# A short product ahead of each sum of products in a hybrid RG-LRU, pooling and Conformer block

## The chip, the cores and the metric

The kernel runs on one core of one Trainium2 chip. The metric is the device time of one execution in microseconds (us). Two runs of the kernel before are shown, 990.06 and 989.09 us; their median is 989.58 us.

## The reference

One layer works on 256 latent tokens and 256 context tokens of 2048 channels. Both are RMS-normalised and modulated by a shift and a scale that come from the condition vectors through `w_ada`. An input projection `w_in` gives seven groups of 1024 columns and three groups of 2048 gate logits:

```python
cols = split(h @ w_in)                        # xa, za, xb, zb, cv, cg, zc, gl
ya = rglru_both_directions(conv4(cols.xa))    # starts from the context's last state
yb = multiscale_pool(cols.xb) ; yc = conformer_conv(cols.cv, cols.cg)   # yc ends in @ w_pwc
acc = sum_k sigmoid(gl[k]) * ((y[k] * silu(z[k])) @ w_bout[k])
out = x + gate * (acc @ w_out + b_out)        # then a last RMS norm over the channels
```

The context takes part only in `xa`. All arithmetic is held to float32, so the kernel writes each operand of a large product as a high and a low part in the format float32r and adds three products: high by high, high by low, low by high.

## The kernel before

The main sequence (the loop `for kind, key, item, q in steps`) is a list of steps, each with one weight piece of 1 MB that the SP queue loads into one of three slots of `raws`. ScalarE writes the high part of a piece (`wh`, line 84) and VectorE the low part (`wl`, line 210), for the next step while TensorE works on this one. Between the splits VectorE runs background chains (convolutions, scan, layer norm, the gate) as far as a step's planned time of 5.1 us has room.

The kinds of steps are: one `xa` step (512 columns of tokens), 48 branch steps (`xb`, `zb`, `cv`, `cg`, `za`, `zc`, eight of each), 48 gate-logit steps (`gl`), 24 projection steps (`bout`), 4 steps of the pointwise convolution (`pwc`) and 16 `out` steps. All but `out` hand their work to one helper, `columns`, as jobs. A job is one sum over k: the weights are the stationary operand, 128 by 128, and the tokens the moving one, 256 columns. For each k it runs the high weights against the high tokens (line 249) and against the low tokens (line 250); when the high parts of all jobs are done, it runs the low weights against the high tokens (line 253). A branch or gate-logit step is one job with 16 values of k, 48 products. A projection step calls `columns` twice, each time with one job of 8 values of k, 24 products. A `pwc` step calls it once with two jobs of 8. The sums of one step go to PSUM banks that ScalarE and VectorE read out in the next step.

Between the steps stand a few other products on TensorE: those of the RG-LRU gates (`mm3`, lines 239 to 241, 512 columns), those of the pooling mixer (`mm3`, 256 columns), and six sums over the partitions with a matrix `ones` in plain float32 (lines 731, 745 and 940). Before the main sequence, phase 1 streams `w_ada` (line 390, 32 stationary columns), turns the sums with products of two columns (lines 398 and 399) and multiplies the first seven tiles of `xa` (`mm3`, 512 columns).

The order on TensorE is the order in which the program emits products; nothing is moved around. The change touches only `columns` and one line of the main loop.

Of the kernel before, what the change touches and what calls it, by code (L numbers as in the profile page):

```python
# [23 lines left out]

# column offsets inside the packed per-channel vectors
V_G, V_BSH, V_BSC = 0, 16, 32
# [6 lines left out]

# arena offsets (float32 per partition)
A_SQ0, A_XT, A_H, A_S, A_RAW = 0, 8192, 16384, 17408, 17920
# [11 lines left out]
class Feed:  # L47
    """Weight pieces of 8 KB per partition: loaded ahead into slots, and split into two float32r parts."""

# [41 lines left out]
class Background:  # L91
    """Elementwise chains cut into small steps that fill the vector engine between weight splits.

    A chain is a list of named generators that run one after another. Each yields None after what it has just
    emitted, "S" where the next part has to wait for the next weight piece, or a function that says whether the
    next part may be emitted (in a tuple where that is only better so)."""

# [7 lines left out]
    def _step(self, chain):  # L105
        """Emits the next part; False if it can't be emitted yet."""
        if chain["until"] is not None:
            if not chain["until"]():
                return False
            chain["until"] = None  # L110
        try:
            r = next(chain["parts"][0][1])
        except StopIteration:
            self.done.add(chain["parts"].pop(0)[0])
            if not chain["parts"]:
                self.chains.remove(chain)
            return True
        chain["soft"] = isinstance(r, tuple)
        if chain["soft"]:
            r = r[0]  # L120
        if callable(r):
            chain["until"] = r
        return r != "S"
# [22 lines left out]
def hybrid_block_kernel(  # L146
# [91 lines left out]
    def mm3(ps, sh, sl, mh, ml, start, stop):  # L238
        T.matmul(ps, sh, mh, start=start, stop=False)  # L239
        T.matmul(ps, sh, ml, start=False, stop=False)  # L240
        T.matmul(ps, sl, mh, start=False, stop=stop)  # L241

    def columns(jobs):
        """Sums over k of weights (stationary) times tokens (moving) in three float32r products each; those
        with the low part of the weights come last, so that it may be late. A job: output, high and low parts
        of the weights per k, high and low parts of the tokens per k."""
        for ps, wh, wl, mh, ml in jobs:
            for k in range(len(wh)):
                T.matmul(ps, wh[k], mh[k], start=k == 0, stop=False)  # L249
                T.matmul(ps, wh[k], ml[k], start=False, stop=False)  # L250
        for ps, wh, wl, mh, ml in jobs:
            for k in range(len(wh)):
                T.matmul(ps, wl[k], mh[k], start=False, stop=k == len(wh) - 1)  # L253

    def tiles128(parts):
        """The 128-column tiles of a split piece, high and low."""
        return [[part[i][:, P * k:P * (k + 1)] for part in parts for k in range(8)] for i in range(2)]

    def rsqrt_newton(o, v, tmp, r):
        """o = 1/sqrt(v): square root, reciprocal, one Newton step."""  # L260
        A.activation(r, v, AF.Sqrt)
        recip(r, r)
        tt(tmp, r, r, ALU.mult)
        tt(tmp, tmp, v, ALU.mult)
        ts(tmp, tmp, -0.5, 1.5)
        tt(o, tmp, r, ALU.mult)

    feed = Feed(nc, whp, wlp)

    # order of the weight pieces  # L270
    main_slots = [(f"m{i}", raws[:, i, :]) for i in range(3)]
# [25 lines left out]
    steps = []  # L297
# [57 lines left out]
    with tc.manual_schedule():  # L355
# [1 line left out]
        cin = sml[:, 0:32]  # L357
# [18 lines left out]
        rows = ar[:, A_RB:A_RB + 512]  # L376
# [41 lines left out]
        def keep_warm(n):  # L418
            """Products that nothing reads: the tensor engine's clock halves when it has been idle."""
            for _ in range(n):  # L420
                T.matmul(warm, ones, xT[:, 10, :], start=True, stop=True)

# [1 line left out]
        fold = ar[:, A_XS:A_XS + 512]  # L424
# [35 lines left out]

# [1 line left out]
        xa_ps = [bank() for _ in range(6)] + [small_bank() for _ in range(NXA - 6)]  # L462
# [18 lines left out]

# [1 line left out]
        xap = [ar[:, A_XAP + 518 * t:A_XAP + 518 * (t + 1)].rearrange("p (s l) -> p s l", s=2) for t in range(8)]  # L483
# [12 lines left out]
        gth = [ar[:, A_GTH + 512 * i:A_GTH + 512 * (i + 1)] for i in range(2)]  # L496
        # context halves of the split modulated tokens, free after xa: products' operands of the branches
        cH, cL = hH[:, :, 256:512], hL[:, :, 256:512]
# [11 lines left out]

# [1 line left out]
        nsp, tsp, brh, bih = sml[:, 96:112], sml[:, 112:128], sml[:, 128:144], sml[:, 144:160]  # L512

        def prep():
            """softplus(-lam) = max(-lam, 0) + log1p(exp(-|lam|)); log1p(e) = 2 atanh(e / (2 + e))."""
            lam = vt[:, V_LAM:V_LAM + 16]
            e, z, q, s = sml[:, 0:16], sml[:, 16:32], sml[:, 32:48], sml[:, 48:64]
            ts(brh, vt[:, V_BR:V_BR + 16], 0.5, None)
            ts(bih, vt[:, V_BI:V_BI + 16], 0.5, None)
            ts(q, lam, -1.0, None)  # L520
            tt(e, lam, q, ALU.min)
            A.activation(e, e, AF.Exp)
            ts(s, q, 0.0, None, op0=ALU.max)
            yield
            ts(z, e, 2.0, None, op0=ALU.add)
            recip(z, z)
            tt(z, z, e, ALU.mult)
            yield
            tt(q, z, z, ALU.mult)
            ts(e, q, 1.0 / 19, 1.0 / 17)  # L530
            for m in (15, 13, 11, 9, 7, 5, 3, 1):
                tt(e, e, q, ALU.mult)
                ts(e, e, 1.0 / m, None, op0=ALU.add)
                yield
            tt(e, e, z, ALU.mult)
            stt(s, e, 2.0, s, ALU.mult, ALU.add)
            ts(nsp, s, -4.0, None)
            ts(tsp, s, 2.0, None)
            yield
            ts(vt[:, V_PS:V_PS + 8], vt[:, V_PS:V_PS + 8], 0.5, None)  # L540
            ts(vt[:, V_CCW:V_CCW + 248], vt[:, V_CCW:V_CCW + 248], 0.5, None)
            ts(vt[:, V_PB:V_PB + 8], vt[:, V_PB:V_PB + 8], 0.5, None)
            yield
# [4 lines left out]
        def conv_a(pr):  # L548
            """Two heads: depthwise convolution of width 4, then the two parts of the result."""
            hd = (2 * pr, 2 * pr + 1)  # L550
# [229 lines left out]

# [1 line left out]
        G.memset(ar[:, A_XAP:A_XAP + 4144], 0.0)  # L782
# [15 lines left out]
        def silu_parts(ps):  # L798
            """(1 + tanh(z / 2)) z, twice silu(z)."""
            th = take("th", th_t)  # L800
            A.activation(th, ps[:, 0:256], AF.Tanh, scale=0.5)
            return th
# [69 lines left out]
        def merge_end(k, j):  # L872
            """Two channel tiles of a branch into the sum; after the last branch, half the sum in two parts."""
            a = acc[:, j, :]
# [29 lines left out]
        def gate_chunk(n):  # L904
            """The gate on every partition: silu(c) times the weight rows of each partition, then the sum over
            the partitions; and x + gate * b_out."""
            c = slice(512 * n, 512 * (n + 1))
# [63 lines left out]
        def finish(t, halves):  # L971
            """The last chunk of a token tile, then the RMS norm over its rows; the first three chunks are
            multiplied by final_g already."""
            var, r, tmp = [sml[:, 16 + 4 * t + i:17 + 4 * t + i] for i in range(3)]
# [25 lines left out]

# [1 line left out]
        first, later, post = [], [], []  # L1002
        step_no = [0]
        avail = load["V"]
        for kind, key, item, q in steps:
# [12 lines left out]
            for f in due:  # L1018
                f()
            parts = it["parts"]  # L1020

            if kind in ("xa", "xb", "zb", "cv", "cg", "za", "zc"):
# [31 lines left out]
            elif kind == "out":  # L1054
# [10 lines left out]
                def out_mm(t, ps, lo, hi, qs, low):  # L1065
                    """One token tile: tokens stationary, weights moving; the low part of the weights last."""
                    tk = slice(P * t, P * (t + 1))
# [60 lines left out]
def _layout(inputs):  # L1128
    """Arrays in the order in which the kernel reads them: permutations, slices and concatenations only."""
    f = {k: np.asarray(v, dtype=np.float32) for k, v in inputs.items()}  # L1130
# [58 lines left out]
```

## Time and profile before

| what | value |
|---|---|
| median of the two runs | 989.58 us |
| span of the profiled execution, first to last instruction | 990.5 us |
| TensorE busy | 965.3 us (97% of the span), 7528 products |
| VectorE busy | 743.6 us (75%) |
| ScalarE busy | 493.0 us (50%) |
| mean granted TensorE clock | 0.993 |
| DMA | 220.70 MB, mean 223 GB/s |

No device time is given for the profiled execution beside its span; the span is 0.9 us over the median of the runs. In the trace a product on TensorE has a record of its own (PE) and so has the load of its weights (PEld). The length of a product's record holds its way through the pipeline and overlaps the next record, so the time that a product really costs is read from start to start, over many products, and is called its pace here.

### The profile page before, as it was taken

The page shows a single profiled execution, that of the slowest core. Times are in us where ns is not written, and L with a number is a line of the kernel's source. Part 1 is how long each engine was busy: PE and PEld are TensorE (multiplying, and loading weights), DVE is VectorE, ACT ScalarE, POOL GpSimd, SP SyncE. Part 2 cuts the span into 40 slices and gives each one's busy share as a digit, 9 for nine tenths or more (in the row PEclk, how much of TensorE's full clock was granted, in tenths as well). Part 3 has the DMA queues.
Part 4 walks back from the last instruction along what each step waited for, and adds up shares of the span by engine and source line. Part 5 has one row for each costly group of instructions (what it writes and reads, how often), then busy time and mean ns, then how long its engine had stood idle before and what let it go on. Part 6 is the DMA issues. An engine that isn't in the chain of part 4 may idle for free.

```text
span 990.5 us, 18090 instructions
## 1 busy us (share of the span) xinstructions
PE 965.3 (97%) x7528; PEld 893.6 (90%) x7528; DVE 743.6 (75%) x1143; ACT 493.0 (50%) x641; POOL 40.6 (4%) x74
## 2 busy tenths in 40 slices
PE   4999999999999999999999999999999999999996
PEld 1566668999999999999999999999999999998885
DVE  5445456866976775889899899896756788998864
ACT  4212226566656767674444533444565464454442
POOL 0000010000100000000000000000002111101000
PEclk9999999999999999999999999999999999999998
DMA  9897854544545555444555545555468789878652
GB/s 373 322 418 313 359 194 162 211 171 167 181 163 182 182 181 178 174 171 170 203 181 176 200 178 191 193 173 175 169 216 342 256 301 331 326 249 303 214 178 85
DMA packets 34722, 220.70 MB, mean 223 GB/s; under 512 B 4128, under 2 KB 4272, under 8 KB 11856
## 3 DMA queue, kind: packets, MB, share of 16 engines
q1 hardware_dynamic: 28080, 195.28, 54.1%
q0 software_dynamic: 6560, 24.26, 7.2%
q8 instruction: 59, 0.97, 0.4%
q14 instruction: 23, 0.19, 0.1%
HBM read 217.43 MB, written 2.10 MB: 222 GB/s over the span
## 4 chain that ended last, share of the span: by engine, by line
PE 96%; DVE 2%; ACT 1%; DMA 1%; issue 0%; ACTq 0%; SPq 0%; DVEq 0%
PE acc L253 24%; PE acc L250 24%; PE acc L249 24%; PE sm L390 3%; PE acc L239 3%; PE acc L1075 3%; PE acc L1077 3%; PE acc L1078 3%; PE acc L240 2%; PE acc L241 2%; DVE ar L210 1%; PE sm L240 1%; PE sm L239 1%; PE sm L241 1%; DMA ar<-in_xt_dram 1%; PE sm L399 0%
## 5 line engine op out<-in xcount | busy, mean ns | idle before, releaser
L249 PE MATMUL acc<-hH,wh 128*128 128x256 f32 (+1 forms) x2000 | 479.2, 282 | 0.0
L250 PE MATMUL acc<-hL,wh 128*128 128x256 f32 (+1 forms) x2000 | 477.7, 281 | 0.0
L84 ACT CAST wh<-raws 128x1024 fp32r<-128x1024 f32 (+1 forms) x288 | 297.8, 1048 | 274.8 <-PE acc L250 186.6
L210 DVE TENSOR_TENSOR wl<-raws,wh 128x1024 fp32r<-128x1024 f32 (+1 forms) x288 | 339.6, 1217 | 120.9 <-issue 58.5
L250 PEld LDWEIGHTS acc<-hL,wh 128*128 128x128 f32 x2000 | 378.0, 189 | 2.1 <-issue 0.7
L249 PEld LDWEIGHTS acc<-hH,wh 128*128 128x128 f32 x2000 | 377.5, 189 | 2.1 <-issue 0.7
L253 PE MATMUL acc<-hH,wl 128*128 128x256 f32 (+1 forms) x2000 | 260.3, 281 | 0.0
L253 PEld LDWEIGHTS acc<-hH,wl 128*128 128x128 f32 x2000 | 245.8, 189 | 0.7
L221 DVE SCALAR_TENSOR_TENSOR ar<-ar,vt 128x256 f32<-128x256 f32 (+1 forms) x264 | 115.2, 501 | 0.0
L210 DVE TENSOR_TENSOR ar<-ar 128x512 f32<-128x512 f32 (+6 forms) x136 | 87.3, 664 | 7.9 <-ACT ar L430 6.2
L221 DVE SCALAR_TENSOR_TENSOR ar<-ar,sc 128x512 f32<-128x512 f32 x64 | 48.0, 750 | 17.5 <-DMA ar<-in_w_gate_dram 16.1
L235 ACT CAST hH<-ar 128x256 fp32r<-128x256 f32 (+1 forms) x68 | 31.5, 491 | 54.2 <-DVE ar L217 46.9
L210 DVE TENSOR_TENSOR hL<-ar,hH 128x256 fp32r<-128x256 f32 (+1 forms) x76 | 39.5, 546 | 23.1 <-ACT hH L235 23.1
L1077 PE MATMUL acc<-wh,hH 128*128 128x512 f32 (+1 forms) x144 | 51.8, 369 | 0.0
L1078 PE MATMUL acc<-wh,hL 128*128 128x512 f32 (+1 forms) x144 | 51.3, 366 | 0.0
L239 PE MATMUL acc<-hH,wh 128*128 128x512 f32 x96 | 42.7, 445 | 1.2 <-ACT hH L235 1.2
L215 DVE TENSOR_SCALAR sml<-sm,vt 128x2 f32<-128x2 f32 x16 | 3.5, 219 | 50.8 <-PE sm L399 50.8
L240 PE MATMUL acc<-hL,wh 128*128 128x512 f32 x96 | 38.6, 403 | 0.3 <-DVE hL L210 0.2
L241 PE MATMUL acc<-hH,wl 128*128 128x512 f32 x96 | 38.4, 400 | 0.0
L239 PEld LDWEIGHTS acc<-hH,wh 128*128 128x128 f32 x96 | 18.2, 190 | 16.1 <-issue 12.0
L1075 PE MATMUL acc<-wl,hH 128*128 128x512 f32 (+1 forms) x144 | 32.1, 366 | 0.0
L1078 PEld LDWEIGHTS acc<-wh,hL 128*128 128x128 f32 x144 | 27.0, 188 | 4.8 <-issue 0.2
(136 smaller groups left out, 649.8 us busy)
## 6 DMA issues: line engine op xcount, KB each, us to landing
raws<-in_w_br_dram SPq DMA_DIRECT2D x49, 1024.0 KB, 4.9
raws<-in_w_gl_dram SPq DMA_DIRECT2D x48, 1024.0 KB, 4.9
raws<-in_w_bout_dram SPq DMA_DIRECT2D x24, 1024.0 KB, 4.9
raws<-in_w_ada_dram SPq DMA_DIRECT2D x16, 1024.0 KB, 8.9
ar<-in_w_ada_dram SPq DMA_DIRECT2D x16, 1024.0 KB, 8.3
ar<-in_w_gate_dram POOLq DMA_DIRECT2D x32, 512.0 KB, 6.6
raws<-in_w_out_dram SPq DMA_DIRECT2D x16, 1024.0 KB, 5.0
ar<-in_w_xa_dram SPq DMA_DIRECT2D x5, 896.0 KB, 11.5
```

The lines of the kernel that those rows point to most:

```text
L84: self.nc.scalar.copy(h[:, 0:w], src)
L210: V.tensor_tensor(out=o, in0=a, in1=b, op=op)
L221: V.scalar_tensor_tensor(o, a, s, b, op0=op0, op1=op1)
L239: T.matmul(ps, sh, mh, start=start, stop=False)
L240: T.matmul(ps, sh, ml, start=False, stop=False)
L241: T.matmul(ps, sl, mh, start=False, stop=stop)
L249: T.matmul(ps, wh[k], mh[k], start=k == 0, stop=False)
L250: T.matmul(ps, wh[k], ml[k], start=False, stop=False)
L253: T.matmul(ps, wl[k], mh[k], start=False, stop=k == len(wh) - 1)
L1075: T.matmul(ps, H, wl[:, w], start=False, stop=kt == KT - 1)
L1077: T.matmul(ps, H, wh[:, w], start=kt == 0, stop=False)
L1078: T.matmul(ps, Lo, wh[:, w], start=False, stop=False)
```

## The change

`columns` gets a switch. While it is on, each job begins with one more product: the first high weight tile against the first n columns of the first high token tile, written to the first n columns of the job's own PSUM area with `start=True, stop=True`. The job's first regular product, with `start=True`, writes the same area anew, so nothing of the short product is left in the sum. The widths n go round through 15 values, from 16 to 240 in steps of 16. The switch is set at every step of the main loop, off for `xa` and on for all others; `out` steps don't call `columns`. Phase 1 is untouched. The diff also empties comments and docstrings, which are left out here.

```diff
+LEADS = (32, 64, 96, 128, 160, 192, 224, 16, 48, 80, 112, 144, 176, 208, 240)
...
+    lead = {"on": False, "i": 0}
+
     def columns(jobs):
         for ps, wh, wl, mh, ml in jobs:
+            if lead["on"]:
+                n = LEADS[lead["i"] % len(LEADS)]
+                lead["i"] += 1
+                T.matmul(ps[:, 0:n], wh[0], mh[0][:, 0:n], start=True, stop=True)
             for k in range(len(wh)):
                 T.matmul(ps, wh[k], mh[k], start=k == 0, stop=False)
                 T.matmul(ps, wh[k], ml[k], start=False, stop=False)
...
             parts = it["parts"]
+            lead["on"] = kind != "xa"
```

## Rows read from the trace of the kernel before

**Rows 1.** The page: busy time, granted clock by slice, shares of the last chain.

```profile
PE 965.3 (97%) x7528; PEld 893.6 (90%) x7528; DVE 743.6 (75%) x1143; ACT 493.0 (50%) x641; POOL 40.6 (4%) x74
...
PEclk9999999999999999999999999999999999999998
...
PE 96%; DVE 2%; ACT 1%; DMA 1%; issue 0%; ACTq 0%; SPq 0%; DVEq 0%
```

**Rows 2.** Waits of PE: line, releaser: us in total, times, longest us.

```profile
PE acc L421 <- DMA ar<-in_xt_dram: 12.7, 1, 12.7
PE acc L239 <- ACT hH L235: 1.2, 1, 1.2
PE acc L443 <- DVE ar L210: 1.0, 1, 1.0
PE sm L390 <- DVE sml L217: 0.4, 1, 0.4
PE acc L240 <- DVE hL L210: 0.2, 1, 0.2
```

**Rows 3.** Groups by line and shape, PE: count | busy us, mean ns | idle.

```profile
L249 PE MATMUL acc<-hH,wh 128*128 128x256 f32 x1984 | 472.9, 281 | 0.0
L250 PE MATMUL acc<-hL,wh 128*128 128x256 f32 x1984 | 471.3, 280 | 0.0
L253 PE MATMUL acc<-hH,wl 128*128 128x256 f32 x1984 | 256.4, 280 | 0.0
```

**Rows 4.** The same view, weight loads (PEld) of line 250.

```profile
L250 PEld LDWEIGHTS acc<-hL,wh 128*128 128x128 f32 x2000 | 378.0, 189 | 2.1 <-issue 0.7
```

**Rows 5.** Windows, PE: from:to us, length, busy (products), clock, DMA share, GB/s.

```profile
163.75:190.95 27.20, 27.20 (x241) 1.00 0.61 217
...
433.71:682.46 248.75, 248.75 (x2113) 1.00 0.53 187
683.02:704.67 21.65, 21.65 (x193) 1.00 0.55 186
705.22:789.90 84.68, 84.68 (x721) 1.00 0.70 250
790.88:834.30 43.42, 43.42 (x386) 1.00 0.83 302
...
875.71:891.92 16.21, 16.21 (x145) 1.00 0.68 222
```

**Rows 6.** Timeline of PE in phase 1: start us, us, line, shape, count.

```profile
49.52 0.39 PE L241 MATMUL acc<-hH,wl 128*128 128x512 f32 x1
49.75 0.28 PE L398 MATMUL sm<-sel,ar 128*128 128x2 f32 x2
49.89 0.36 PE L399 MATMUL sm<-sel,ar 128*128 128x2 f32 x2
50.11 0.48 PE L239 MATMUL acc<-hH,wh 128*128 128x512 f32 x1
50.43 0.39 PE L240 MATMUL acc<-hL,wh 128*128 128x512 f32 x1
50.66 0.40 PE L241 MATMUL acc<-hH,wl 128*128 128x512 f32 x1
50.90 0.39 PE L239 MATMUL acc<-hH,wh 128*128 128x512 f32 x1
```

**Rows 7.** Timeline of PE: the first of twelve pooling products, the product after them.

```profile
190.96 0.28 PE L239 MATMUL acc<-hH 128*128 128x256 f32 x1
...
192.39 0.28 PE L249 MATMUL acc<-hH,wh 128*128 128x256 f32 x1
```

**Rows 8.** Timeline of PE: float32 products of `ones` between the windows.

```profile
682.46 0.60 PE L731 MATMUL acc<-ar,ones 128*128 128x256 f32 x2
...
704.67 0.59 PE L745 MATMUL acc<-ar,ones 128*128 128x256 f32 x2
...
789.90 1.02 PE L940 MATMUL acc<-ar,ones 128*128 128x512 f32 x2
```

## The prediction

> **What bounds the kernel now.** I read the page first. TensorE is busy for 97% of the span, the chain that ended last is 96% TensorE, and the granted clock stands at full speed in nearly all slices [rows 1]. The view of waits says where TensorE is not busy: five waits, 12.7 + 1.2 + 1.0 + 0.4 + 0.2 = 15.5 us, all on lines of phase 1 [rows 2]. The steps that the change touches hold no idle time of TensorE (0.0 at each of their three groups [rows 3]). So the kernel is a queue of products, and a product added there lengthens it by what it costs; nothing hides it, and no other engine's wait is ahead of it. The short product needs the weights, the tokens and the PSUM area that the product behind it needs anyway, so it adds no wait of its own. VectorE, ScalarE and the weight loads from memory get more time per step than they have now.
>
> The view that decides is the one that gives the pace of the products. Lines 249, 250 and 253 run 3 x 1984 = 5952 products of 256 columns [rows 3]. Their records are 280 ns long and overlap, so I take windows that begin and end with a product's start and hold these products alone, and divide (the count of a window includes the one or two records that reach into it; steps of 48 give the exact one). The result is not one pace but two [rows 5]. From 433.71 to 682.46 us 2112 products take 248.75 us, 117.8 ns each; 705.22 to 789.90 gives the same (84.68 us by 719). From 163.75 to 190.95, 240 products take 27.20 us, 113.3 ns each; so do the windows from 683.02 (191), 790.88 (383) and 875.71 (143). Instructions, shapes and clock (1.00, which is 2.4 GHz) are the same in both. The pace holds for tens of microseconds and changes only where something else stood between the sums: the twelve pooling products, which themselves go at (192.39 - 190.96) / 12 = 119 ns and leave the slow pace behind them [rows 7], or one float32 product with `ones`, at 682.46 (slow to fast), 704.67 (fast to slow), 789.90 (slow to fast) [rows 8]. The fast windows hold 240 + 192 + 384 + 144 = 960 products, whole steps counted; I count the other 4992 as slow. The difference is 4.45 ns a product.
>
> **The change part by part.** It removes and moves nothing. It adds one product to each sum: 48 branch sums, 48 gate-logit sums, 2 x 24 projection sums and 2 x 4 of the pointwise convolution, together 152. Their widths are ten full rounds of the 15 values (1920 columns) and 32 + 64, in all 19296 columns, 127 on average.
>
> What one costs. Every product has a weight load of its own: line 250 loads 2000 times [rows 4], although line 249 just ahead of it used the same tile, so the regular product behind the short one will load again. What a product costs when there is next to nothing to stream is shown in phase 1: from 49.52 to 50.43 us stand two products of 512 columns and four of two columns [rows 6]. The next two products of 512 columns take 50.90 - 50.43 = 0.47 us, so the four short ones take 0.91 - 0.47 = 0.44 us, 110 ns each. That is close to a full product of 256 columns, and the width does not matter up to 240 columns: at the fast pace a column streams in 113.3 / 256 = 0.443 ns, and 240 take 106 ns. I take the pace of the sum that the product leads, 113 to 118 ns, since that row is a plain float32 one and the neighbours are float32r: 152 x 115.6 = 17.6 us. The bounds are 152 x 110 = 16.7 us and, at the pooling products' 119 ns, 18.1 us. The lower end would go to the columns alone, 19296 x 0.443 = 8.5 us, if the second load of the same weights were hidden; that is a rival below.
>
> By the Trainium skill, "TensorE: Matmul & The Clock Gate", section "Back-to-back issue gap", an isolated product of N columns takes N / 2.4 + 2.5 ns, which is an estimate of 152 x 55 = 8.4 us here; the two-column products in the trace disagree with it as a price for products that each load weights.
>
> What it does to the pace. This is the unknown. Each short product is a disturbance like those that changed the pace before: for one product the load of the weights and the streaming are out of step, and the widths make the disturbance different from sum to sum. No row shows a short float32r product of this kind. The bounds are that all 5952 products go fast (4992 x 4.45 = 22.2 us less) and that all go slow (960 x 4.45 = 4.3 us more). Since the disturbances in the trace went both ways (fast to slow at 704.67, slow to fast at 682.46 and 789.90), and since the widths differ, I take half the sums fast and half slow: 2976 slow instead of 4992, 2016 x 4.45 = 9.0 us less.
>
> The sum: 17.6 - 9.0 = +8.6 us on the profiled execution, whose span of 990.5 us is 0.9 us over the median of the runs; on the median that is 989.6 + 8.6 = 998 us.
>
> By the Trainium skill, the same page, "Step-by-step: what each phase is for", TensorE has two independent read ports and loading the next weights doesn't steal bandwidth from the running product; by that there would be nothing for a short product to shift. The two paces of the same instructions in the trace speak against reading it so strictly.
>
> **The rivals.**
>
> *The pace stays as it is.* What flips the pace may be a plain float32 product only, with its longer streaming, and not a short one. For it: the pace is the same on both sides of the border between many steps. Against it: nothing stands between those sums now. It gives 989.6 + 152 x 117.1 ns (17.8 us) = 1007 us.
>
> *Every short product drops its sum into the slow pace* (the other side). Its place is the first load after it, which then cannot start early. For it: after the two-column products of phase 1 the 512-column ones go at 0.47 / 2 = 235 ns [rows 6], over twice 113.3. It costs 152 x 117.8 = 17.9 us and 4.3 us for the 960 products that lose the fast pace: 1012 us. It decides, past 2%, from the point where fewer than some 530 products (9%) stay fast. A worse form of it is the pooling products' 119 ns for everything: 18.1 + 4992 x 1.2 ns + 960 x 5.7 ns = 29.6 us, 1019 us.
>
> *Every short product leaves the fast pace.* For it: after the wide products of `xa`, at 163.75, the stream went straight to 113.3 ns [rows 5]. It gives 989.6 + 152 x 113.3 ns (17.2) - 22.2 = 985 us: the products cost less than the order they bring.
>
> *The short product costs only its columns.* The load that follows is of the same weights and might be gone behind the streaming. It gives +8.5 us and, with half the sums fast, 989 us; with the pace as before, 998 us; with all fast, 976 us. Against it: rows 6.
>
> That the change does not do what it says, the 152 products being dropped as unread, I give no chance of its own: phase 1 runs products into `warm` that nobody reads, and they are in the trace.
>
> **How the numbers follow.** A measurement of this kernel can tell about 2% (20 us) from no change, so the borders are 970 and 1009 us. Chances: mixed paces 0.45 (998 us, its own range 991 with three quarters fast to 1005 with one quarter); pace as before 0.17 (1007); all slow 0.14 (1012); all at the pooling pace 0.05 (1019); all fast 0.12 (985); columns only 0.07 (976 to 1002). The prediction is the first case's, 998 us. The range 987 to 1013 leaves out all fast (0.12), the pooling pace (0.05) and the low part of the last case (0.03). Slower by over 2% are all slow and the pooling pace, 0.19. Faster by over 2% is out of reach of every case: even all fast with columns only stays at 976; I leave 0.01. The rest, 0.80, is within 2%.
>
> **What would show it.** In the changed trace TensorE should have 7680 products. The short ones should form groups of 152 in all, and the step from the start of one sum to the start of the next should be 49 paces long where it was 48: a branch step 5.55 us if fast and 5.77 us if slow, against 5.44 and 5.65 us now. Windows over whole steps should show both paces, changing at the short products. If the step is longer by much less than 110 ns at the same pace, the price is wrong; if all windows show one pace, the mixture is. The prediction is wrong as a whole if TensorE starts to wait for ScalarE, VectorE or a weight piece in these steps, or if a third pace appears that no row here has.

## The result, and the profile after

The changed kernel takes 1000.52 us (median of two runs, 999.75 and 1001.29), against 989.58 us before: the ratio is 1.0111, with a 95% interval from 1.0082 to 1.0141. It is 10.9 us slower; 8.6 us were forecast.

The page and the waits of TensorE of the changed kernel (lines moved by two to nine, so line 257 is the former 249, 258 the 250, 261 the 253, and 255 is the short product):

```profile
span 999.5 us, 18397 instructions
PE 974.6 (98%) x7680; PEld 903.8 (90%) x7680; DVE 744.2 (74%) x1143; ACT 493.2 (49%) x641; POOL 40.6 (4%) x74
...
PE acc L429 <- DMA ar<-in_xt_dram: 12.9, 1, 12.9
PE acc L241 <- ACT hH L237: 1.2, 1, 1.2
PE acc L451 <- DVE ar L212: 0.5, 1, 0.5
PE sm L398 <- DVE sml L219: 0.4, 1, 0.4
```

There are 7680 products where there were 7528, each with a load of its own, and TensorE waits nowhere but in phase 1, as in [rows 2]. So all that was added is in the queue of products. Next, the stretch from the first product of `columns` to the first one of the `out` steps, as windows of PE with the columns of [rows 5], first before, then after:

```profile
152.55:891.92 739.37, 739.37 (x6155) 1.00 0.59 206
```

```profile
150.81:900.83 750.02, 750.02 (x6307) 1.00 0.58 204
```

The stretch grew by 10.65 us, nearly the whole of the 10.9 us between the medians. (The profiled span grew by 9.0 us only, because phase 1 ended 1.7 us earlier in this execution.)

Where the 10.65 us lie is seen sum by sum. One gate-logit and four branch steps of the changed kernel in a row, each window from one short product to the next, so 49 products each; the two or three records more that a window counts overlap its edges. The widths are 224, 16, 48, 80 and 112:

```profile
732.20:737.75 5.55, 5.55 (x51) 1.00 0.55 187
737.75:743.51 5.76, 5.76 (x51) 1.00 0.55 196
743.51:749.28 5.77, 5.77 (x51) 1.00 0.52 182
749.28:754.85 5.57, 5.57 (x52) 1.00 0.54 185
754.85:760.40 5.55, 5.55 (x52) 1.00 0.95 342
```

At 113.3 ns the 48 regular products take 5.44 us, at 117.8 ns 5.65 us. So the first sum is fast with a short product of 0.11 us, the next two are slow with the same 0.11 us, the fourth turns from slow to fast and pays 0.13 us, the fifth is fast. The pace, which in [rows 5] held for tens of microseconds, now changes from sum to sum. Read this way from the start of each product, 66 of the 152 sums, 2632 of the 5952 products, are fast and 3320 slow, where 960 and 4992 were so before. A short product costs 119 ns on average, counted until the pace behind it has settled, some five products on (147 of them; five stand behind float32 products and can't be told apart): 110 ns where the sum behind it goes slow (84), 113 ns from fast to fast (9), 136 ns where a slow stream turns fast (39), 128 ns where a fast sum follows products of another kind (15). That gives 152 x 119 ns = 18.1 us for the short products and (4992 - 3320) x 4.45 ns = 7.4 us back for the pace: +10.7 us, the 10.65 us of the stretch. Each count of fast and slow products here and below is that of one profiled execution.

What a short product costs does not follow its width. Two starts in the changed kernel, a product of 16 and one of 112 columns (the timeline of PE, start first):

```profile
737.75 0.17 PE L255 MATMUL acc<-hH,wh 128*128 128x16 f32 x1
737.78 0.36 PE L257 MATMUL acc<-hH,wh 128*128 128x256 f32 x1
737.98 0.28 PE L258 MATMUL acc<-hL,wh 128*128 128x256 f32 x1
...
754.85 0.21 PE L255 MATMUL acc<-hH,wh 128*128 128x112 f32 x1
754.90 0.34 PE L257 MATMUL acc<-hH,wh 128*128 128x256 f32 x1
755.07 0.28 PE L258 MATMUL acc<-hL,wh 128*128 128x256 f32 x1
```

The narrower the short product, the sooner the one behind it starts by the record (0.03 and 0.05 us) and the longer it is from there to the next start (0.20 and 0.17 us). Together it is 0.23 and 0.22 us, two full products. The weight loads at the first of these places (PEld):

```profile
737.64 0.19 PEld L255 LDWEIGHTS acc<-hH,wh 128*128 128x128 f32 x1
737.75 0.19 PEld L257 LDWEIGHTS acc<-hH,wh 128*128 128x128 f32 x1
737.86 0.19 PEld L258 LDWEIGHTS acc<-hL,wh 128*128 128x128 f32 x1
```

Line 257 loads its weights anew, though line 255 had the same ones, and the loads start 0.11 us apart, however little is streamed between them. In none of the traces do two loads of 128 columns start less than 108 ns apart. So the short product takes a place of its own in the row of loads. That the load itself sets this time, and not another fixed cost of a product, is read from these starts; no run has a short load together with a short stream.

### The profile page after: what moved, and what is told of

The parts are those of the page before. It is cut to its first block, busy times and chain, and to the rows that moved or that the text cites. A ratio compares the mean times of both kernels' runs of the same rounds, so it can differ in the third digit from the quotient of the medians.

```text
span 999.5 us, 18397 instructions
## 1 busy us (share of the span) xinstructions
PE 974.6 (98%) x7680; PEld 903.8 (90%) x7680; DVE 744.2 (74%) x1143; ACT 493.2 (49%) x641; POOL 40.6 (4%) x74
## 4 chain that ended last, share of the span: by engine, by line
PE 96%; DVE 2%; DMA 1%; ACT 1%; issue 0%; SPq 0%; ACTq 0%; DVEq 0%
PE acc L257 24%; PE acc L258 23%; PE acc L261 23%; PE acc L241 3%; PE sm L398 3%; PE acc L1084 3%; PE acc L1086 3%; PE acc L1087 3%; PE acc L242 2%; PE acc L243 2%; PE sm L242 1%; DVE ar L212 1%; PE sm L241 1%; PE sm L243 1%; PE acc L255 1%; DMA ar<-in_xt_dram 1%
## 5 line engine op out<-in xcount | busy, mean ns | idle before, releaser
L255 PE MATMUL acc<-hH,wh 128*128 128x32 f32 (+4 forms) x152 | 35.2, 232 | 0.0
```

## The experiments

Each experiment starts from the kernel before and adds short products in its own way; the times of the kernel before are those of the same chip.

**One width for all, 112 columns.**

```diff
             if lead["on"]:
+                T.matmul(ps[:, 0:112], wh[0], mh[0][:, 0:112], start=True, stop=True)
```

> All 152 short products 112 columns wide. Theory (the width, with the pace the stream comes from, decides which pace follows): in the changed kernel's trace all ten sums behind a 112-column product went at the fast pace, from either pace, so nearly all 5952 products go at 113.3 ns. 989.6 + 152 x 0.114 (17.3) - 22.2 = 985 us. Rival (a short product re-draws the pace by chance, whatever its width): about half the sums fast, 1000 us. Second rival (the pace pays no heed to these products and the price is all): 1007 us.

Measured: 985.80 us against 991.62, ratio 0.9936 (0.9917 to 0.9954). All 152 sums are fast. Ten sums in a row and the whole stretch:

```profile
500.57:556.10 55.53, 55.53 (x492) 1.00 0.54 189
149.36:883.98 734.62, 734.62 (x6308) 1.00 0.60 208
```

55.53 / 490 is 113.3 ns. The same number of added products that made the kernel slower makes it faster when they all have this width, so what decides is the pace that they leave behind. The account closes: 152 x 114.7 ns (17.4 us) less 22.2 us is -4.8, and the stretch is 739.37 - 734.62 = 4.75 us shorter. Chance, and price alone, fall.

**One width for all, 48 columns, and later 16.** The same edit with 48, then with 16.

> All 152 short products 48 columns wide. Theory: nine of ten sums behind a 48-column product were slow in the changed kernel's trace (the tenth stood behind the RG-LRU products), so only sums behind those are fast, some 16 of 152. 989.6 + 152 x 0.111 (16.9) + about 1 us for the fast stretches that are lost = 1007 to 1009 us, some 22 us over the 112-column version. Rival (chance, whatever the width): 1000 us and no difference from the 112-column version.

> All 152 short products 16 columns wide. In the changed kernel a 16-column product turned the pace over in all nine sums that stood right behind another sum (six slow to fast, three fast to slow). Theory (the step from one pace to the next follows from the width and the pace before): fast and slow sums alternate, about half the products fast, 989.6 + 152 x 0.12 (18) - 9 = 998 us. Rival (the nine were chance): runs of equal pace, share anywhere; or the stream settles on one pace for good, 986 or 1010 us.

Measured: 1003.63 us against 991.62 with 48 columns, ratio 1.0118 (1.0099 to 1.0137); 1003.65 us against 990.05 with 16 columns (one run each). Both expectations of the theory were off: 49 of the 152 sums are fast with 48 columns, not some 16, and with 16 columns the paces don't alternate. What came instead is more regular than the theory. Five sums in a row with 48 columns, then the same five with 16:

```profile
519.56:525.13 5.57, 5.57 (x51) 1.00 0.57 181
525.13:530.89 5.76, 5.76 (x51) 1.00 0.56 201
530.89:536.66 5.77, 5.77 (x52) 1.00 0.49 179
536.66:542.42 5.76, 5.76 (x51) 1.00 0.48 176
542.42:548.00 5.58, 5.58 (x52) 1.00 0.51 185
```

```profile
519.81:525.39 5.58, 5.58 (x52) 1.00 0.54 182
525.39:531.15 5.76, 5.76 (x51) 1.00 0.54 195
531.15:536.91 5.76, 5.76 (x51) 1.00 0.52 181
536.91:542.68 5.77, 5.77 (x52) 1.00 0.53 190
542.68:548.25 5.57, 5.57 (x51) 1.00 0.51 178
```

One sum at the fast pace, three at the slow pace, one at the fast, and so on; and over all 152 sums the two kernels have the same sequence of fast and slow, in two profiles and with two widths. So 16 and 48 columns are one and the same disturbance here, and the slow pace behaves as if it were three states, through which the stream is moved step by step until it is fast for one sum. The cycle of four holds wherever nothing of another kind stands between, with one exception: the eight sums of the `pwc` steps go fast, slow, fast, slow in both kernels, and the runs don't show why. In the changed kernel 16 columns had turned the pace over each time; there they always stood behind 224 columns, and the present run shows that the width alone doesn't do it.

**As wide as the regular products, 256 columns.**

> The additional product is as wide as the regular ones, 256 columns. It separates the price from the shift: a product like its neighbours should not disturb the stream, so the windows keep the two paces where they were before. Theory: 989.6 + 152 x 0.117 = 1007 us, paces as before, switching at the products of the pooling, the RG-LRU and the float32 sums alone. Rival (it is the additional product as such, a reload of the same weights or a start flag, that shifts the pace, and not its width): paces mixed sum by sum, 1000 us.

Measured: 1008.65 us against 991.62, ratio 1.0166 (1.0149 to 1.0183). The paces stay where they were but in the first five sums behind `xa`: 5232 products are slow, 4992 before. These five are slow from their first product, and the difference lies ahead of it. The 512-column products of `xa` start 231 and 236 ns apart by turns, and the last step, to the first product of 256 columns, is 235 ns in the profile of the kernel before and 231 ns in this one, though both kernels emit the same products up to there. (Of the ten kernels profiled, three end `xa` on 235 or 236 ns and seven on 230 or 231.) So the stream can leave `xa` in either of two positions, and the order of the products alone does not fix which. The window between the two float32 products that bound 705.22 to 789.90 in [rows 5]:

```profile
717.36:804.28 86.92, 86.92 (x741) 1.00 0.68 246
```

The window holds 738 products, 18 of them added, and 86.92 / 738 is 117.8 ns, as before. A product like its neighbours costs 117.3 ns and shifts nothing in the windows that can be compared; it is not the reload of the same tile or the start flag that shifts the pace. The price without the shift is 152 x 117.3 ns = 17.8 us, and with it 240 x 4.45 ns = 1.1 us: together the 18.9 us by which the stretch grew (758.26 us).

**112 columns, only where something else came between.** The switch is set by `mm3` and behind the three lines with products of `ones` (one is shown), and the next sum of 256 columns clears it; 24 short products are left.

```diff
     def mm3(ps, sh, sl, mh, ml, start, stop):
+        lead["on"] = True
...
             T.matmul(ps[:, 0:256], ones, tree[:, 0:256], start=True, stop=True)
+            lead["on"] = True
...
+            if lead["on"] and ps.shape[-1] == 256:
+                lead["on"] = False
+                T.matmul(ps[:, 0:112], wh[0], mh[0][:, 0:112], start=True, stop=True)
```

> A 112-column product only ahead of the first sum after a product of another kind (RG-LRU, pooling, float32 sums, phase 1), some 27 in all, none elsewhere. Theory: the fast pace holds until something else comes between, so one product after each such place is enough: 989.6 - 22.2 + 27 x 0.12 (3.2) = 971 us. Rival (the fast pace lasts only while each sum is led anew): the sums without a short product fall back, 985 to 990 us. Second rival (price alone counts): 993 us.

Measured: 972.89 us against 991.62, ratio 0.9804 (0.9782 to 0.9827), 19 us faster than the kernel before, and by the two ratios 3% faster than the change. All 5952 products are at the fast pace. The long stretch between the last RG-LRU product and the first float32 product, 433.71 to 682.46 in [rows 5], and the whole stretch:

```profile
425.87:665.35 239.48, 239.48 (x2114) 1.00 0.56 194
150.60:871.70 721.10, 720.35 (x6180) 1.00 0.61 211
```

239.48 us hold 2112 products and one short one, 113.3 ns each, where the same took 248.75 us. One short product at its head is enough for 44 steps: the fast pace holds by itself. The account: -22.2 us, 24 x 124 ns = 3.0 us, and a wait of 0.75 us ahead of a float32 product, which was not there before: -18.5 us; the stretch is 18.3 us shorter.

**Two of 112 columns in a row**, ahead of every sum.

> Two 112-column products in a row ahead of every sum, to measure the price alone. Theory (each pays about one weight load, whatever it streams): 152 x 112 ns = 17.0 us more than with one, 1003 us, if the second one leaves the fast pace as the first does; up to 22 us more on top if two shift the pace back. Rival (a product costs its columns, 112 x 0.443 = 50 ns, and the first one's price was a one-off of the change of weights): 7.5 us more, 993 us.

Measured: 1008.42 us against 989.17, ratio 1.0185 (1.0156 to 1.0215). The stretch takes 757.94 us, 23.3 us more than with one. 1056 products went back to the slow pace (4.7 us); the rest is 18.6 us or 122 ns for each second product. The rival, 50 ns by the columns, is off by more than a factor of two. With two at the head, all 113 sums that follow a fast one directly stay fast, but only 5 of the 15 that follow a slow one directly turn fast.

**144 columns, only where something else came between.** The same 24 places.

> As the version with 112 columns only where a product of another kind came before, but 144 columns wide. Theory (the width decides): behind 144 columns ten of ten sums were slow in the changed kernel, so all is slow: 991.6 + 4.3 + 24 x 0.115 (2.8) = 999 us. Rival (any short product at these places sets the stream straight): 972 to 974 us as with 112.

Measured: 979.39 us against 989.17, ratio 0.9889 (0.9867 to 0.9911): neither 999 nor 972 us. The windows behind the RG-LRU products (first) and between the float32 products, which begin one product late, behind the short one:

```profile
424.62:664.04 239.42, 239.42 (x2115) 1.00 0.56 193
664.53:687.19 22.66, 22.66 (x194) 1.00 0.52 180
687.70:772.42 84.72, 84.72 (x721) 1.00 0.71 251
773.78:819.06 45.28, 45.28 (x387) 1.00 0.84 302
```

Behind the 19 places with RG-LRU, pooling or `xa` products the stream is fast (113.4 ns in the first window), behind all five float32 products it is slow (117.8 ns). In the changed kernel 144 columns were followed by a slow sum ten times of ten, nine of them behind a fast sum. So a width has no pace of its own: what stood before it counts as much.

**All 256 columns, but a load of 32.** The additional product has 32 weight columns and fills 32 partitions of its area.

```diff
             if lead["on"]:
+                T.matmul(ps[0:32, 0:256], wh[0][:, 0:32], mh[0][:, 0:256], start=True, stop=True)
```

> The additional product streams all 256 columns but its weights are 32 columns of the tile (its output is 32 partitions of the area), so its load is short and its streaming is not. With all 256 columns and the full load the paces stayed as before. Theory (a product shifts the pace when its streaming ends before the next load does, and here it does not): paces as with 256 columns, price 0.113 to 0.118 us each, 1008 us. Rival (any mismatch of load and streaming shifts it): the paces mix or go to one side, between 986 and 1003 us or over 1010 us.

Measured: 988.44 us against 989.17, ratio 0.9988 (0.9976 to 1.0001). The expectation fell, the rival held: with a full stream and a short load (its record is 108 ns long, a regular one's 188) the paces shift too, and to the fast side. 5160 products are fast: all 128 sums that stand right behind another sum, whichever pace that one had, as with 112 columns; the 19 slow sums all stand behind products of another kind. Ten sums in a row:

```profile
503.29:558.82 55.53, 55.53 (x493) 1.00 0.55 190
```

152 products at 116.5 ns (17.7 us) buy (4992 - 792) x 4.45 = 18.7 us. Of the additional products tried, the one that is exactly like the regular ones is the only one that left the pace alone.

## Why the prediction was right

**The bound.** TensorE without a wait, everything added in its queue: held. No other engine's wait appeared, and the stretch of the sums carries nearly the whole difference (10.65 of 10.9 us).

**The price.** 115.6 ns were taken, the mean of the two paces, after the 110 ns of the two-column products in [rows 6]; 119 ns were measured, and the two-in-a-row kernel shows 122 ns for each second product. The rival that a short product costs only its columns (8.5 us) is out: 18.1 us. That the price does not follow the width held; it goes from 109 to 148 ns by what happens to the pace, and the dear ones are those behind which the sum goes fast without having been so before. The working kept price and pace apart; here the turn to the fast pace is paid for in the price.

**The two paces.** The reading of [rows 5] carried the argument, and the fully fast kernel showed the 22.2 us that it set as the most to be gained. The counts of 960 and 4992 are those of one execution; the profile with 256 columns shows that the first 240 can be slow as well, which is worth 1.1 us. The share was taken as one half for want of a row; it was 44%, 7.4 us instead of 9.0 us. With the price (18.1 us instead of 17.6) that is the difference between +8.6 and +10.65 us.

**Why one half.** Here the number was better than the reason. The step of the working that took the short products for disturbances that go both ways, with another result for each sum, was a description and not a mechanism. The runs speak against chance: two kernels gave the same 152 paces in a row, and 112 columns gave one pace only. That the change stood near the middle fits with fifteen widths that move the stream through its states in different steps; the step of each width was not worked out, so why it came to 44% is not shown. That one half lay so near is luck.

**The other rivals.** "Every short product drops its sum into the slow pace" was weighed on the 512-column products behind the two-column ones in [rows 6]; narrow products do leave most sums slow (16 and 48 columns, 103 of 152), but not all, and 1012 us were not reached by any single width tried. "Every short product leaves the fast pace" is true of 112 columns, where its 5 us less came out as 5.8 us less, but not of the fifteen widths. It was weighed on the stream that went straight to 113.3 ns behind `xa`; in the profile with 256 columns the same place is slow. "The pace stays as it is", 17.8 us more, is what 256 columns do (17.0 us more).

**What stays open.** The runs show that the pace is a state that TensorE's stream carries on from product to product, and that products unlike their neighbours in streaming or in load can move it. It does not go with the DMA traffic: in [rows 5] the windows at 113.3 ns have DMA shares from 0.55 to 0.83, those at 117.8 ns 0.53 and 0.70. That the same order of products moves it in the same way each time is shown only as far as the two sequences with 16 and 48 columns agree; each kernel was profiled once, and the end of `xa` shows that what comes in can differ. What this state is in the hardware, a position of the load against the streaming or something else, the runs don't show. No record says which of three slow states a sum is in; that there are three is read from the sequence alone, and the `pwc` steps don't fit it.

## What to carry to other kernels

Where TensorE is the bound, divide windows of like products by their count, stretch by stretch: a pace that differs between stretches with the same instructions is time that may be had without removing any work. Here one short product ahead of the first sum behind each product of another kind, 24 in all, was worth 2%, while 152 of mixed widths cost 1%; which width does it has to be tried in place, since it depends on what stands before. An additional product in this stream cost about a full one, however narrow it was.

## What was not expected of the hardware

Products of 256 columns with 128 by 128 weights ran at 113.3 or 117.8 ns at the same granted clock (1.00), and either pace lasted, up to 2112 products and 249 us, until another kind of product came. Additional products of 16 and of 48 columns had the same effect on all 152 sums, outside the `pwc` steps in a cycle of one fast and three slow. A product with a quarter of the weights and all the columns cost 116.5 ns, as much as a full one, and one with all the weights and 16 to 240 columns cost 109 to 148 ns.
